# The place of two operand transpositions among the steps of an RWKV-7 scan on TensorE

## The chip, the cores and the metric

The kernel runs on one core of a Trainium2 chip. The metric is the device time of one execution in microseconds (us). TensorE (PE in the profile; PEld is its loading of weights) multiplies matrices into PSUM, VectorE (DVE) and ScalarE (ACT) work on the elements and copy out of PSUM, GpSimd (POOL) works on SBUF, and SyncE (SP) issues the transfers. Each engine works through its own instructions strictly in the order in which the program has them, and waits on semaphores for the others.

## The reference, cut to what matters

The program is a decoder trunk of two layers on 512 tokens of width 2048, all in 32-bit floats. Layer 0 has stick-breaking attention and a pooling mixer; layer 1 is RWKV-7 time mixing with 32 heads of 64. The part that the change touches is the recurrence of layer 1:

```python
def step(state, inp):
    r_t, w_t, k_t, v_t, kk_t, a_t = inp
    sa = jnp.einsum('bhvk,bhk->bhv', state, -kk_t)
    state = (state * w_t[:, :, None, :]
             + sa[..., None] * (kk_t * a_t)[:, :, None, :]
             + v_t[..., None] * k_t[:, :, None, :])
    return state, jnp.einsum('bhvk,bhk->bhv', state, r_t)
...
r = (xr @ w_r); k = (xk @ w_k); v = (xv @ w_v); g = (xg @ w_g)
...
o = wkv7_scan(r, decay, k, v, kk, a)
...
return o.astype(x.dtype) @ w_o
```

## The kernel before, in words

Layer 0, and the projections r, k and g of layer 1, take about the first 1430 us. Then comes the scan, which is what the change edits. It handles the 32 heads as 16 pairs and the 512 tokens as 8 chunks of 64. Within a chunk the recurrence becomes dense products. For each pair `p` the code has generators, whose pieces end at each `yield`:

- `chain(p)` is the serial part. Per chunk it has three steps: `xo` from the running state `M` and the operands (L1044, L1047) and its copy to `xs` by DVE and ACT (L1051, L1052); the product `sa` of `U` and `xs` (L1055) and its copy into `RS` by DVE (L1056); then `s1` (L1062) from `RS` and `BT`, the new state `M` by DVE (L1071, L1073) and the second half of `xo` (L1076).
- `gprod(p)` prepares a pair: it loads the operands `AR` and `BK` (L898, L900, 512 KB each), makes the products `g` of both (L908) and masks them into `Z` (L914) in four pieces, and transposes the eight blocks of `BK`, four at a time (`bt`, L920), each four copied into `BT` by ACT (L921). These last two pieces are the two transpositions of the title. `BK` has one buffer, so the load for the next pair waits until the second transposition of this pair has read it. `AR` has four buffers.
- `lanes(p)` inverts small blocks, almost wholly on DVE: `nd` by POOL (L950), its transposition `lt` (L955), `la` (L957), then fifteen steps of a product `pr` and a sum `uc` (L962, L963). `levels(p)` joins the blocks on TensorE (`q`, `c`: L1000, L1010) with additions into `U` (L1013, L1026).
- `vproj(p)` is the projection v of the pair, 512 columns wide (`vps`, L145 to L147 by a helper), its weights arriving as `wraw` (L154) and being split by ACT and POOL; `vprep(p)` transposes v (L937); `post(p)` normalises the output and multiplies by the gate.

The pieces are laid out in time by hand. A period has twelve positions, and one pair is begun in each period. In each position, `slot` first runs one step of each of the two chains that are alive, and then all pieces whose due time falls in that position. Since each chain takes three positions for a chunk, positions 0, 3, 6 and 9 hold `xo`, positions 1, 4, 7 and 10 hold `sa`, and positions 2, 5, 8 and 11 hold `s1`. The tuple `GP = (0.5, 9)` spreads the six pieces of `gprod` evenly over that stretch: at 0.5, 1.9, 3.3, 4.75 (the products g), 6.2 and 7.6 (the two transpositions). TensorE's order is exactly the written one; the orders of DVE, ACT, POOL and SP come out of a scheduler that works by priority and by what it reckons to be ready.

The first two pairs are prepared ahead of the loop; the other fourteen go through `plan_pair`.

Of the kernel before, what the change touches and what calls it, by code (L numbers as in the profile page):

```python
# [27 lines left out]

PO, LA, VP, LV, GP, VJ = (13.5, 20), (8, 15), (21.5, 25), (16, 24.5), (0.5, 9), (5.5, 17)
Q14, A13, B13, A14, B14, A15, B15, Q15 = (0, 3), (0.5, 5.5), (6, 12), (0, 10), (3, 12), (0, 9), (0.5, 11.5), (0, 11.5)


class Kernel:
# [809 lines left out]
    def scan(self, ctx, xv, first, mp, ld, ar_d, bk_d, bc_d, g_d, m_d):  # L845
# [29 lines left out]
        def vproj(p):  # L875

            unit = lambda k0: self.wunit(
                Wv[k0 * P:(k0 + 4) * P, p * P:(p + 1) * P].rearrange("(k p) n -> p k n", p=P), 4, P,
                eng=nc.gpsimd if p > 1 else None)
            ws = first if p == 0 else [unit(0)]  # L880
            ps = pv.tile([P, S], F32, tag="v", name="vps")
            for k in range(NK):
                if k % 4 == 0:
                    wh, wl = ws.pop(0)
                    if k + 4 < NK and not ws:
                        ws.append(unit(k + 4))
                self.mm3(ps, wh[:, k % 4, :], wl[:, k % 4, :], xv[k][:, 0, :], xv[k][:, 1, :], k == 0, k == NK - 1)
                if k % 2 and k < NK - 1:
                    yield
            vT = sets[p]["vT"] = tp.tile([P, S], F32, tag="vT", name="vT")  # L890
            nc.scalar.copy(vT, ps)  # L891
            yield

        def gprod(p):

            s = sets[p]
            AR = s["AR"] = ld.tile([P, 8, 2, 64], F32, tag="AR", name="AR", bufs=4)
            nc.sync.dma_start(AR.rearrange("p a b c -> p (a b c)"), ar_d[p])  # L898
            BK = ld.tile([P, 8, P], F32, tag="BK", name="BK")
            nc.sync.dma_start(BK.rearrange("p a b -> p (a b)"), bk_d[p])  # L900
            yield

            Z = s["Z"] = [st.tile([P, 8, P], F32, tag=f"Z{h}", name=f"Z{h}", bufs=4) for h in range(2)]
            for b in range(2):
                g = [aux("g").rearrange("p (c n) -> p c n", c=4) for _ in range(2)]
                for c in range(4):
                    for h in range(2):
                        mm(g[h][:, c, :], BK[half[h], 4 * b + c, :],  # L908
                           AR[half[h], 4 * b + c].rearrange("p a b -> p (a b)"), start=True, stop=True)
                    if c == 1:  # L910
                        yield
                for h in range(2):
                    mk = self.mk[:, 64 * (p % 2):64 * (p % 2) + P]
                    nc.vector.tensor_mul(Z[h][:, 4 * b:4 * b + 4, :], g[h], mk.unsqueeze(1).to_broadcast([P, 4, P]))  # L914
                yield
            BT = s["BT"] = st.tile([P, 8, P], F32, tag="BT", name="BT")
            for b in range(2):
                g = aux("bt")
                for c in range(4):
                    nc.tensor.transpose(g[:, c * P:(c + 1) * P], BK[:, 4 * b + c, :], self.ident)  # L920
                nc.scalar.copy(BT[:, 4 * b:4 * b + 4, :], g.rearrange("p (c n) -> p c n", c=4))  # L921
                yield

        def vprep(p):

            s = sets[p]
            bv = s["bv"] = tp.tile([P, S], F32, tag="bv", name="bv", bufs=3)
            nc.sync.dma_start(bv, bc_d[p])
            for q in range(4):
                nc.gpsimd.tensor_mul(bv[:, q * P:q * P + P], s["vT"][:, q * P:q * P + P], bv[:, q * P:q * P + P])  # L930

            RS = s["RS"] = st.tile([P, 8, 2, 64], F32, tag="RS", name="RS", bufs=3)
            nc.gpsimd.memset(RS[half[p % 2]], 0.0)
            yield
            g = aux("vt")
            for t in range(4):
                nc.tensor.transpose(g[:, t * P:(t + 1) * P], s["vT"][:, t * P:(t + 1) * P], self.ident)  # L937
            g5 = g.rearrange("p (t h n) -> p t h n", t=4, h=2)
            for par, rows in ((0, lo), (1, hi)):
                nc.scalar.copy(RS[half[1 - p % 2], par::2], g5[rows])  # L940
            yield
# [217 lines left out]
        todo = []  # L1159

        def plan(base, g, n, a, b):

            todo.extend((base + a + (b - a) * q / n, len(todo), g) for q in range(n))
# [12 lines left out]
        def hurry(g):  # L1176
            while True:
                with tc.high_priority(offset=400):
                    if next(g, g) is g:
                        return  # L1180
                yield

        def plan_pair(base, q, skip=0):

            gp = gprod(q)
            next(gp)
            plan(base, gp, 6, *GP)
            plan(base, hurry(lanes(q)) if q == 15 else lanes(q), 18, *LA)
            plan(base, hurry(levels(q)) if q == 15 else levels(q), 5, *LV)
            plan(base, vproj(q), 8, *VJ)  # L1190
            plan(base, vprep(q), 2, *VP)


        v, gp = vproj(0), gprod(0)
# [33 lines left out]
        for p in range(-1, 16):  # L1228
            at = 12 * (p + 1)
            if p + 3 < 16:  # L1230
                plan_pair(at, p + 3)
            if 0 <= p < 15:
                late = 1.2 if p in (13, 14) else 0
                plan(at, post(p), 6, PO[0] + late, PO[1] + late)
            if p == 13:
                plan(at, units(0, 1, 2), 3, *A13)
                plan(at, project(*both(0, 1, 2)), 6, *B13)
            if p == 14:
                plan(at, units(3, 4, 5, 6, 7), 5, *A14)
                plan(at, project(*both(3, 4, 5, 6, 7)), 10, *B14)  # L1240
                plan(at, project(*[(2, k) for k in range(3)]), 3, *Q14)
            if p == 15:
                plan(at, units(8, 9, 10, 11, 12, 13), 6, *A15)
                plan(at, project(*both(8, 9, 10, 11, 12, 13)), 12, *B15)
                plan(at, project(*[(2, k) for k in range(3, 10)]), 7, *Q15)
            B = chain(p + 1) if p < 15 else None
            slot(at, [c for c in (A, B) if c])
            A = B
# [91 lines left out]
```

## Time and profile before

| | us |
|---|---|
| median of three runs | 2084.72 |
| lowest and highest of them | 2082.19, 2085.89 |
| the profiled execution | 2082.21 |
| its span, first to last instruction | 2080.4 |
| TensorE busy in it | 2016.8 (97%) |
| VectorE busy | 1282.0 (62%) |
| ScalarE busy | 961.5 (46%) |
| GpSimd busy | 282.7 (14%) |

Between the span and the time of the execution lie 1.8 us. The shares are means over stages with different limits: most of the span is the large projections, in which TensorE never waits. A timeline row gives the start, the duration from the first to the last of the merged instructions, the engine, the line, the operation, the tiles (out<-in) with their sizes, the count, and in brackets the idle time ahead of it and who ended it.

### The profile page before, as it was taken

The numbers are of one execution on the slowest core, as the hardware profiler recorded it, in microseconds if no ns is written. First come the engines' busy times: TensorE is split into PE (matmuls) and PEld (weight loads), VectorE is DVE, ScalarE is ACT, GpSimd is POOL, SyncE is SP. The second block draws the span as 40 slices with busy tenths as digits, with TensorE's granted clock in tenths as the row PEclk, the third lists the DMA queues.
The fourth block names the chain that finished last, engine by engine and source line by source line (L and its number), as shares of the span: only waits on it lengthen the run. The fifth ranks groups of instructions, "written<-read, shape, count | busy, mean of one in ns | idle before, by whom it ended". The sixth has DMA issues, their size and how long they took to land.

```text
span 2080.4 us, 33934 instructions
## 1 busy us (share of the span) xinstructions
PE 2016.8 (97%) x13091; PEld 1637.4 (79%) x13091; DVE 1282.0 (62%) x2572; ACT 961.5 (46%) x1687; POOL 282.7 (14%) x550
## 2 busy tenths in 40 slices
PE   8999999999999998999999999999999999989996
PEld 7888888888888897777878888886777777767786
DVE  5344345444433357666866676668788888886436
ACT  3345445323322138654745564454555555564221
POOL 0000000000000000234000000013444444410003
PEclk9999999999999999999999999999999999999998
DMA  5222222233333353465365556542223332232733
GB/s 195 92 81 81 81 81 66 86 97 100 98 111 112 115 169 126 138 180 178 118 213 190 181 171 218 198 166 67 91 76 106 109 108 89 95 118 92 245 105 111
DMA packets 214034, 262.99 MB, mean 126 GB/s; under 512 B 15769, under 2 KB 161777, under 8 KB 213105
## 3 DMA queue, kind: packets, MB, share of 16 engines
q1 hardware_dynamic: 213872, 260.83, 38.6%
q8 instruction: 103, 1.69, 0.3%
q14 instruction: 59, 0.48, 0.1%
HBM read 214.32 MB, written 46.47 MB: 125 GB/s over the span
## 4 chain that ended last, share of the span: by engine, by line
PE 77%; DVE 14%; ACT 3%; issue 2%; DMA 2%; POOL 1%; SPq 0%; DVEq 0%; ACTq 0%; POOLq 0%
PE ga L145 16%; PE ga L146 16%; PE ga L147 16%; PE gb L506 4%; PE gb L508 4%; PE gb L507 4%; DVE pr L962 2%; PE vps L145 2%; DVE uc L963 1%; DVE M L1071 1%; PE vps L146 1%; PE vps L147 1%; DVE RS L1056 1%; PE g L908 1%; PE y L506 1%
## 5 line engine op out<-in xcount | busy, mean ns | idle before, releaser
L141 DVE TENSOR_TENSOR wlo<-wraw,whi 128x1024 fp32r<-128x1024 f32 (+1 forms) x268 | 314.1, 1175 | 467.3 <-ACT whi L137 464.0
L137 ACT CAST whi<-wraw 128x1024 fp32r<-128x1024 f32 (+1 forms) x324 | 303.0, 938 | 545.2 <-PE ga L146 297.9
L145 PE MATMUL ga<-mx,whi 128*128 128x512 f32 x768 | 299.9, 391 | 3.2 <-ACT mx L137 3.2
L146 PE MATMUL ga<-mx,whi 128*128 128x512 f32 x768 | 300.4, 391 | 1.6 <-DVE mx L141 1.6
L145 PE MATMUL ga<-x,whi 128*128 128x512 f32 x768 | 300.5, 391 | 0.1
L147 PE MATMUL ga<-mx,wlo 128*128 128x512 f32 x768 | 300.3, 391 | 0.0
L147 PE MATMUL ga<-x,wlo 128*128 128x512 f32 x768 | 299.5, 390 | 0.5 <-DVE wlo L141 0.5
L146 PE MATMUL ga<-x,whi 128*128 128x512 f32 x768 | 299.2, 390 | 0.0
L508 PE MATMUL gb<-wlo,mixed 128*128 128x512 f32 (+1 forms) x576 | 197.4, 344 | 2.8 <-DVE wlo L141 2.8
L506 PE MATMUL gb<-whi,mixed 128*128 128x512 f32 (+1 forms) x576 | 198.0, 344 | 1.6 <-DVE s L457 1.6
L507 PE MATMUL gb<-whi,mixed 128*128 128x512 f32 (+1 forms) x576 | 197.5, 343 | 0.0
L145 PEld LDWEIGHTS ga<-mx,whi 128*128 128x128 f32 x768 | 144.8, 189 | 36.3 <-ACT mx L137 3.6
L146 PEld LDWEIGHTS ga<-mx,whi 128*128 128x128 f32 x768 | 144.9, 189 | 32.9 <-DVE mx L141 1.9
L147 PEld LDWEIGHTS ga<-mx,wlo 128*128 128x128 f32 x768 | 144.8, 189 | 30.6
L147 PEld LDWEIGHTS ga<-x,wlo 128*128 128x128 f32 x768 | 144.2, 188 | 31.2 <-DVE wlo L141 1.0
L145 PEld LDWEIGHTS ga<-x,whi 128*128 128x128 f32 x768 | 144.2, 188 | 29.6 <-ACT whi L137 0.4
L146 PEld LDWEIGHTS ga<-x,whi 128*128 128x128 f32 x768 | 144.3, 188 | 29.1
L141 POOL TENSOR_TENSOR wlo<-wraw,whi 128x128 fp32r<-128x128 f32 x224 | 100.3, 478 | 221.9 <-ACT whi L137 195.1
L508 PEld LDWEIGHTS gb<-wlo,mixed 128*128 128x128 f32 x576 | 109.4, 190 | 16.4 <-DVE wlo L141 3.7
L506 PEld LDWEIGHTS gb<-whi,mixed 128*128 128x128 f32 x576 | 109.5, 190 | 16.0 <-DVE s L457 3.3
L507 PEld LDWEIGHTS gb<-whi,mixed 128*128 128x128 f32 x576 | 109.6, 190 | 12.5
L145 PE MATMUL vps<-mx,whi 128*128 128x512 f32 x256 | 113.4, 443 | 0.8 <-ACT vT L891 0.8
(333 smaller groups left out, 3347.7 us busy)
## 6 DMA issues: line engine op xcount, KB each, us to landing
wraw<-in_ev_w_in SPq DMA_DIRECT2D x96, 512.0 KB, 3.6
wraw<-in_ev_w_out SPq DMA_DIRECT2D x32, 512.0 KB, 3.6
wraw<-in_od_w_k SPq DMA_DIRECT2D x32, 512.0 KB, 4.7
wraw<-in_od_w_r SPq DMA_DIRECT2D x32, 512.0 KB, 3.4
wraw<-in_od_w_g SPq DMA_DIRECT2D x32, 512.0 KB, 3.8
wraw<-in_od_w_v SPq DMA_DIRECT2D x64, 256.0 KB, 2.8
ar_d<-pAR SPq DMA_DIRECT2D x16, 512.0 KB, 2.6
bk_d<-pBK SPq DMA_DIRECT2D x16, 512.0 KB, 3.2
```

The source lines that it names most:

```text
L137: self.nc.scalar.copy(hi, src)
L141: (eng or self.nc.vector).tensor_sub(lo[:, sl], src[:, sl], hi[:, sl].bitcast(F32))
L145: mm(ps, ah, bh, start=start, stop=False)
L146: mm(ps, ah, bl, start=False, stop=False)
L147: mm(ps, al, bh, start=False, stop=stop)
L506: mm(ps, ah, bh, start=start, stop=False)
L507: mm(ps, al, bh, start=False, stop=False)
L508: mm(ps, ah, bl, start=False, stop=stop)
L908: mm(g[h][:, c, :], BK[half[h], 4 * b + c, :], AR[half[h], 4 * b + c].rearrange("p a b -> p (a b)"), start=True, stop=True)
L962: nc.vector.tensor_mul(q, uc[:, :t, :t], la[:, t, :t].unsqueeze(1).to_broadcast([P, t, t]))
L963: nc.vector.tensor_reduce(uc[:, :t, t], q, AX.X, ALU.add)
L1056: nc.vector.tensor_copy(RS[a, c], sa[a])
```

## The change

`GP` becomes a list of six times, one for each piece, instead of a stretch. The four products g keep their positions (0, 1, 3 and 4). The first transposition goes from position 6 to position 7 (it was due at 6.2, now at 7.6), and the second from position 7 to position 10 (from 7.6 to 10.5).

```diff
-PO, LA, VP, LV, GP, VJ = (13.5, 20), (8, 15), (21.5, 25), (16, 24.5), (0.5, 9), (5.5, 17)
+PO, LA, VP, LV, GP, VJ = (13.5, 20), (8, 15), (21.5, 25), (16, 24.5), (0.5, 1.9, 3.3, 4.75, 7.6, 10.5), (5.5, 17)
...
             gp = gprod(q)
             next(gp)
-            plan(base, gp, 6, *GP)
+            todo.extend((base + x, len(todo), gp) for x in GP)
             plan(base, hurry(lanes(q)) if q == 15 else lanes(q), 18, *LA)
```

On TensorE, position 6 of a period, the difference between the two programs (- is before, + is changed; bt is the transposition, vps the v projection behind it):

```order
 L1047 MATMUL xo<-RS,Z_11009 64x64
 L1047 MATMUL xo<-RS,Z_11151 64x64
-L920 MATMUL bt<-ident,BK 128x128 x4
 L145 MATMUL vps<-mx,whi 128x512
 L146 MATMUL vps<-mx,whi 128x512
```

The four blocks that stood between xo and the v projection are gone from there. Position 7 reads the same in both programs (sa, c, four blocks bt, s), only that these are now the first four blocks of the pair and no longer the last.

On TensorE, position 10 of the same period (sa of the two chains, c a product of levels):

```order
 L1055 MATMUL sa<-xs_10977,U 64x128
 L1055 MATMUL sa<-xs_10978,U 64x128
-L1000 MATMUL c_12086<-U,q_12053 32x32 x16
+L920 MATMUL bt<-ident,BK 128x128 x4
+L1000 MATMUL c_12086<-U,q_12047 32x32 x16
 L1062 MATMUL s_12105<-RS,BT 64x64 x2
 L1076 MATMUL xo<-RS,Z_11008 64x64
```

Four blocks now stand between sa and c. Both differences come fourteen times, once for each pair that `plan_pair` places.

On SP, which issues the transfers, from the gate's load ldg on, in one period before:

```order
L1087 DMA ldg<-g_d 128x512
L900 DMA BK<-bk_d 128x1024
L898 DMA AR<-ar_d 128x1024
L154 DMA wraw<-in_od_w_v 128x4x128 x4
```

and in the same place of the changed program:

```order
L1087 DMA ldg<-g_d 128x512
L154 DMA wraw<-in_od_w_v 128x4x128
L898 DMA AR<-ar_d 128x1024
L900 DMA BK<-bk_d 128x1024
L154 DMA wraw<-in_od_w_v 128x4x128 x3
```

The load of BK has gone behind one load of weights and behind that of AR. DVE's and ACT's rows are laid out anew by the scheduler too: on ACT the second copy BT stands behind the position's cast whi; on DVE the steps pr and uc lie differently around the copies xs, RS and M, by one or two steps either way. POOL's order is the same.

## Rows read from the trace of the kernel before

**Rows 1.** The page: busy us of each engine, share of the span, instructions.
```profile
PE 2016.8 (97%) x13091; PEld 1637.4 (79%) x13091; DVE 1282.0 (62%) x2572; ACT 961.5 (46%) x1687; POOL 282.7 (14%) x550
```

**Rows 2.** Windows, the scan: us, then busy of PE, PEld, DVE, ACT, POOL, granted clock.
```profile
1430.00:1830.00 400.00, 384.14 (x4889) 288.19 (x4889) 341.33 (x1107) 229.79 (x591) 172.25 (x340) 1.00 0.30 95
```

**Rows 3.** Waits of PE from 1430 to 1830: total us, times, longest.
```profile
PE s L1062 <- DVE RS L1056: 8.8, 22, 0.7
...
PE c L1000 <- ACT q L1021: 0.3, 1, 0.3
```

**Rows 4.** Timeline of PE, positions 6 and 7 of one period.
```profile
1585.44 0.65 PE L920 MATMUL bt<-ident,BK 128*128 128x128 f32 x4
1585.85 0.48 PE L145 MATMUL vps<-mx,whi 128*128 128x512 f32 x1
...
1587.42 0.44 PE L1055 MATMUL sa<-xs,U 128*64 128x128 f32 x4
...
1588.63 0.66 PE L920 MATMUL bt<-ident,BK 128*128 128x128 f32 x4
1589.21 0.45 PE L1062 MATMUL s<-RS,BT 128*64 128x64 f32 x8
```

**Rows 5.** Timeline of PE, position 10 and on: typical, first, last, and behind c.
```profile
1594.45 0.44 PE L1055 MATMUL sa<-xs,U 128*64 128x128 f32 x4
1594.82 0.69 PE L1000 MATMUL c<-U,q 32*32 32x32 f32 x32
1596.23 0.34 PE L1062 MATMUL s<-RS,BT 128*64 128x64 f32 x4 [0.72 <-DVE RS L1056]
...
1599.31 0.72 PE L908 MATMUL g<-AR,BK 64*128 64x128 f32 x8
...
1480.59 0.34 PE L1062 MATMUL s<-RS,BT 128*64 128x64 f32 x4 [0.65 <-DVE RS L1056]
...
1802.27 0.34 PE L1062 MATMUL s<-RS,BT 128*64 128x64 f32 x4 [0.36 <-DVE RS L1056]
...
1831.45 0.54 PE L1000 MATMUL c<-U,q 32*32 32x32 f32 x22 [0.67 <-ACT q L1021]
```

**Rows 6.** Timeline of ACT and DVE and PE, position 6 of two neighbouring periods.
```profile
1585.74 0.71 DVE L955 STREAM_TRANSPOSE lt<-nd 128x512 f32<-128x512 f32 x1 [1.63 <-POOL nd L950]
1586.65 0.47 ACT L1052 COPY xs<-xo 64x64 f32<-64x64 f32 x2 [1.14 <-DVE xs L1051]
...
1616.61 0.45 ACT L1052 COPY xs<-xo 64x64 f32<-64x64 f32 x2 [1.56 <-DVE xs L1051]
...
1616.97 0.59 PE L1055 MATMUL sa<-xs,U 128*64 128x128 f32 x4
```

**Rows 7.** Landing: BK in 1400-1420, 1440-1480, 1500-1800; AR in 1500-1800.
```profile
DMA to landing us min/median/max: 3.4/3.5/3.6
...
DMA to landing us min/median/max: 3.6/3.8/4.1
...
DMA to landing us min/median/max: 4.4/5.1/5.6
...
DMA to landing us min/median/max: 4.0/4.8/5.8
```

**Rows 8.** Timeline of SP, the loads of one period.
```profile
1588.90 0.41 SPq L1087 DMA_DIRECT2D ldg<-g_d  x1
1589.37 0.42 SPq L900 DMA_DIRECT2D BK<-bk_d  x1
1591.89 0.32 SPq L898 DMA_DIRECT2D AR<-ar_d  x1
```

**Rows 9.** Timeline of PE, later waits of s for RS; ACT at position 11.
```profile
1632.40 0.28 PE L1062 MATMUL s<-RS,BT 128*64 128x64 f32 x2 [0.28 <-DVE RS L1056]
1639.53 0.28 PE L1062 MATMUL s<-RS,BT 128*64 128x64 f32 x2 [0.19 <-DVE RS L1056]
1596.84 0.54 ACT L1079 COPY O<-xo 64x128 f32<-64x128 f32 x2 [1.22 <-PE xo L1076]
```

## Prediction

> **What bounds the kernel now.** I read the page first: TensorE is busy 97% of the span, so whatever moves the end must be idle time of TensorE or work added to it [rows 1]. Then the windows: in the scan, from 1430 to 1830 us, TensorE is busy 384 of 400 us and DVE 341, at a granted clock of 1.00 [rows 2]. So 16 us are all that could be gained there, and DVE is close behind. The list of waits says whom TensorE waits for: 8.8 us in 22 waits of s for RS, which DVE copies, and 0.3 us of c for ACT's q [rows 3]. Last I read the timeline where blocks bt are taken out and put in. Ten of the 22 waits stand at position 10, right behind c; read from the timeline they come to 5.9 us, the first 0.65, the last 0.36, most 0.5 to 0.74 [rows 5]. Positions 6 and 7 show no wait of TensorE [rows 4].
>
> **The change, part by part.** The number of instructions stays the same everywhere; only places change.
>
> Out of position 6. The four blocks set back the next work by 1585.85 - 1585.44 = 0.41 us [rows 4], 14 x 0.41 = 5.7 us. But what follows the v projection there is sa, which needs xs from ACT. In the period at 1585, ACT's copies end at 1586.65 + 0.47 = 1587.12 and sa starts at 1587.42 [rows 4, 6]: no more than 0.30 us can be taken. In the neighbouring period they end at 1616.61 + 0.45 = 1617.06 while sa has begun at 1616.97, and takes 0.59 instead of 0.44 us because its second half waits [rows 6]: nothing can be taken. xs is late because DVE must first do lt, which stood 1.63 us waiting for POOL's nd [rows 6], and no transposition moves nd. In the trace six periods are like the first, five like the second, and three early ones have room for the whole 0.41. That is 6 x 0.30 + 3 x 0.41 = 3.0 us gained; the other 2.7 us turn into new waits of sa for xs.
>
> Position 7 holds sa, c, four blocks and s, as before: nothing.
>
> Into position 10. Ahead of s, four blocks cost 1589.21 - 1588.63 = 0.58 us [rows 4], 14 x 0.58 = 8.1 us. They fill the wait behind them: of the ten waits for RS seven are longer than 0.58 and give 4.1 us, the other three (0.52, 0.29, 0.36) give 1.2; in two periods it is c that waits for q, 0.30 us in one and 0.67 in the other [rows 3, 5], which gives 0.9. Together 6.1 us, so that position 10 costs 8.1 - 6.1 = 2.0 us net. The longer stay in position 10 delays nothing that DVE needs earlier than now, since s starts within 0.1 us of its old time in the typical period: 1594.45 + 0.37 + 0.58 + 0.69 = 1596.09 against 1596.23.
>
> ACT's copy BT goes with the blocks. It falls into the 1.22 us in which ACT idles ahead of O [rows 9], and costs nothing; if that cover were gone, O and the copies of v behind it would be late by one such copy, and with them the products g that reuse their PSUM.
>
> The load of BK. This is the wait that the change adds. BK has one buffer, and its load starts when the last blocks have been read. Before, that was 1588.63 + 0.66 = 1589.29 [rows 4]; SP issued at 1589.37 [rows 8], and g needed it at 1599.31 [rows 5], 9.9 us later. Now the blocks end 0.37 + 0.66 = 1.03 us after sa of position 10 starts, and SP, which will be standing at this load, issues some 0.03 us later. g is due after 0.37 + 0.58 + 0.69 us for sa, bt and c, and 1599.31 - 1596.23 = 3.08 us from s to g [rows 5], thus 4.72 us after that start. So the load has 4.72 - 1.06 = 3.66 us. Behind it on SP are only loads of weights, which wait for POOL's splits anyway, and behind g on TensorE stand v's projection, sa and everything else. How long does it take? With little else on the way 3.4 to 4.1 us (four loads); with the transfers m_d and ldg issued within a microsecond ahead of it 4.4 to 5.6, median 5.1 (eleven); and AR, issued 2.5 us behind BK, took 4.0 to 5.8 [rows 7, 8]. In the new order AR goes out some 3.6 us ahead and ldg over 6 us ahead, so the nearest rows are the first four. I take 3.8 us, toward their upper end: g then waits 0.14 us, 13 times (the last pair has no load behind it), 1.8 us. About half of that comes back, since in half the periods s waits for RS twice after g, 0.28 and 0.19 us [rows 9], and DVE sets those times: 0.9 us remain. The ends are 0 (3.66 us or less) and, at 5.1 us, a wait of 1.44 us, of which even with 0.47 given back 13 x 0.97 = 12.6 us are lost.
>
> The Trainium skill, "DMA: Bandwidth & Descriptors", section "Issuing engines are not separate DMA queues", says that all transfers run on the same 16 DMA engines and interleave. Here 512 KB took 3.4 us with the queue clear and 5.1 us in company, which agrees. By that rule AR's tail would stretch BK too, and the term would lie nearer to 12.6 than to 0.9 us.
>
> DVE's and ACT's new order. The steps pr and uc are the same work; they shift by one or two places, in some periods with RS earlier, in four with la or a step ahead of xs. Nothing in the trace shows this order. I cost it at nothing, between -3 us (the 8.8 us of waits for RS less the 5.9 at position 10) and +5 us (a wait like that of 0.72 us [rows 5] once in every second of the fourteen periods).
>
> Sum: -3.0 + 2.0 + 0.9 = -0.1 us. The profiled execution took 2082.21 us, 1.8 of them outside its span of 2080.4, which the change does not touch; it lies 2.5 us under the median of the runs. From its own time the sum gives 2082.1, from the median 2084.6. I predict 2084.6 us: no change. Within 0.2%, 4 us, this kernel's runs cannot tell a change from none.
>
> **Rivals.** The first ends on the slower side: the load of BK comes too late in every period. Mechanism: a single buffer, freed at position 10, needed at position 12. It decides from the point where the load takes about 4.5 us: then g waits 1.06 + 4.5 - 4.72 = 0.84 us, 0.37 after what DVE gives back, 4.8 us over 13 periods; at 5.1 us it is 12.6 us. Its middle is +9 us, 2094 us. For it: eleven of the fifteen loads in the scan took 4.4 us or more [rows 7]. Against it: those had ldg right ahead of them [rows 8], and the new place has not.
>
> The Trainium skill, "Perfetto Trace Analysis", section "Optimization Strategy", names this as a pattern: the same gap repeated on the engine that should be saturated can mean too few buffers for the next tile. No run here shows it yet.
>
> The second: the gain comes whole. If the new order on DVE brings xs and RS to TensorE in time, position 6 gives its 5.7 us, position 10 costs only 2.0, and of the remaining 2.9 us of waits for RS 2 go as well: -5.7 + 2.0 - 2.0 = -5.7 us, 2079 us. For it: in most periods of the new order RS at position 10 stands ahead of one more step pr or uc. Against it: DVE runs without a gap from lt to the next period, so a copy made earlier makes a step later, and lt itself hangs on POOL [rows 6].
>
> The third: time only changes its place. TensorE's wait goes from position 10 to position 6, and BK's load lands just in time: between -3 and +3 us. This is my forecast's own case, with DVE as the pace.
>
> **How the numbers follow.** No change, with the load in time or nearly: 0.55, its own range 2081 to 2089. BK late: 0.23, from 2089 to 2100. Gain whole: 0.17, from 2077 to 2081. DVE's order costing 5 us by itself: 0.05. Slower by over 0.2% is BK late and the bad order, less the part of the former under 4 us: 0.26. Faster by over 0.2% is the whole gain and a small tail of the main case: 0.19. Within: 0.55. The range for 8 in 10 cuts a tenth at either end: 2079 to 2096 us.
>
> **What the profile would show.** Right: s at position 10 no longer waits for RS; new waits of sa for xs at position 6, about 0.1 us (0.41 - 0.30) in one kind of period and 0.4 in the other; BK issued about 1 us after sa of position 10 starts and landing 3.5 to 4 us later; g at position 0 waiting 0.2 us at most; the scan from 1430 to 1830 as long as before. Wrong: g waiting for BK by half a microsecond or more in each period, or position 6 without waits and a scan shorter by over 4 us.

## The result, and the profile after

The changed kernel is slower: a median of 2091.76 us in 13 runs (2087.46 to 2096.65), against 2082.19 us for the kernel before in its 13 runs of the same comparison. The ratio is 1.0047, 95% interval [1.0037, 1.0057], that is 7.7 to 11.9 us. The forecast was no change, 2084.6; the time lies in its range, on the side of the rival with the late load. The profiled execution happens to be the slowest of the 13, 2096.65 us with a span of 2094.9. So a second execution was profiled as well (2091.32 us, span 2089.6), which stands for the typical one.

The page of the changed kernel, busy us of each engine, answers to [rows 1]:

```profile
PE 2026.8 (97%) x13091; PEld 1643.3 (78%) x13091; DVE 1286.2 (61%) x2572; ACT 962.7 (46%) x1687; POOL 281.8 (13%) x550
```

The number of instructions is the same, yet TensorE is busy 10.0 us longer. The same matmuls took longer, and the windows say most of why. First the scan, in the profiled execution, then in the second one (columns as in [rows 2]; the third figure from the end is the granted clock):

```profile
1430.00:1830.00 400.00, 380.48 (x4689) 284.44 (x4688) 333.98 (x1070) 222.79 (x570) 164.22 (x325) 0.98 0.29 90
```

```profile
1430.00:1830.00 400.00, 381.12 (x4765) 284.53 (x4765) 338.35 (x1080) 226.24 (x581) 168.50 (x332) 1.00 0.30 91
```

Before, the clock was 1.00 there and TensorE busy 384.14 us [rows 2]. So two things were added: waits, in both executions, and a lower clock, far more in the slower one.

The waits of TensorE from 1430 to 1830 us in the profiled execution (total us, times, longest) answer to [rows 3]:

```profile
PE g L908 <- DMA BK<-bk_d: 6.1, 5, 2.5
PE q L1000 <- ACT DT L973: 3.7, 3, 1.6
PE s L1062 <- DVE RS L1056: 3.0, 9, 0.6
PE sa L1055 <- ACT xs L1052: 2.8, 5, 1.6
PE vps L145 <- ACT vT L891: 2.4, 4, 0.8
```

and the lines of the kernel before that the prediction had not shown beside [rows 3]:

```profile
PE q L1000 <- ACT DT L973: 2.3, 4, 0.6
PE sa L1055 <- ACT xs L1052: 1.8, 3, 1.3
...
PE vps L145 <- ACT vT L891: 0.8, 1, 0.8
```

Read as a balance, s no longer waits for RS at position 10 and c no longer for q: 8.8 + 0.3 - 3.0 = 6.1 us less. In exchange g waits 6.1 us for BK, and q, sa and vps wait 8.9 us for ACT instead of 4.9. That is 4 us more waiting in the scan, and it is made of other waits: of the 22 short ones, none over 0.7 us, 9 are left, and longer ones have come. In the second execution the list reads 4.2 us for BK in five waits, the longest 1.2, and the same 3.7, 2.8 and 2.4 us for DT, xs and vT.

A period with its load in time shows the two moves as the prediction drew them. This is TensorE's timeline at position 7 and then 10 of one pair, to the next pair's first g, answering to [rows 4, 5]:

```profile
1626.83 0.44 PE L1055 MATMUL sa<-xs,U 128*64 128x128 f32 x4
1627.20 0.91 PE L1010 MATMUL c<-U,q1z 64*48 64x32 f32 x32
1628.04 0.65 PE L920 MATMUL bt<-ident,BK 128*128 128x128 f32 x4
...
1633.86 0.44 PE L1055 MATMUL sa<-xs,U 128*64 128x128 f32 x4
1634.23 0.65 PE L920 MATMUL bt<-ident,BK 128*128 128x128 f32 x4
...
1635.43 0.34 PE L1062 MATMUL s<-RS,BT 128*64 128x64 f32 x4
...
1638.50 0.79 PE L908 MATMUL g<-AR,BK 64*128 64x128 f32 x8
```

None of these rows carries a wait. The period's first g starts at 1609.25 (its row below), so it took 29.25 us; the same one before took from 1599.31 [rows 5] to 1628.79, 29.48. It is 0.23 us shorter, where the forecast's -3.0 + 2.0 makes 0.07 a period: the sign agrees, and one period shows no more. Nor is it free of waits: s waits 0.23 us for RS and vps 0.69 for vT, where before q waited 0.57 for DT and s 0.52 for RS.

What differs more is a few periods that go wrong. Here the load of BK takes its time, and what follows costs on top of the wait (columns of the timeline; in brackets the idle time ahead and its releaser):

```profile
1576.74 1.32 PE L908 MATMUL g<-AR,BK 64*128 64x128 f32 x8 [2.50 <-DMA BK<-bk_d]
1577.99 0.79 PE L145 MATMUL vps<-mx,whi 128*128 128x512 f32 x1
1578.58 0.63 PE L146 MATMUL vps<-mx,whi 128*128 128x512 f32 x1
1579.01 0.63 PE L147 MATMUL vps<-mx,wlo 128*128 128x512 f32 x1
...
1609.25 0.79 PE L908 MATMUL g<-AR,BK 64*128 64x128 f32 x8
...
1610.31 0.39 PE L146 MATMUL vps<-mx,whi 128*128 128x512 f32 x1
1610.54 0.40 PE L147 MATMUL vps<-mx,wlo 128*128 128x512 f32 x1
```

Eight products g take 1.32 us instead of 0.79, and the products vps follow each other at 0.43 us instead of 0.23: half speed, 1.2 instead of 2.4 GHz. The windows of the same execution put the clock to it, behind the five waits of 1.16 (xo for M, at 1434), 1.63 (sa for xs, 1472), 2.50, 1.31 (q for DT, 1592) and 1.58 us (q for DT, 1742):

```profile
1436.00:1440.00 4.00, 3.99 (x23) 3.10 (x24) 2.14 (x5) 0.66 (x2) 1.76 (x3) 0.59 0.03 6
...
1474.00:1478.00 4.00, 4.00 (x26) 3.02 (x26) 3.68 (x14) 1.51 (x4) 1.02 (x3) 0.57 0.22 66
1576.00:1580.00 4.00, 3.26 (x13) 2.68 (x14) 1.31 (x7) 0.40 (x2) 0.00 (x0) 0.58 0.01 4
1592.00:1596.00 4.00, 4.00 (x54) 3.55 (x55) 2.16 (x5) 1.55 (x4) 2.21 (x4) 0.71 0.22 64
1596.00:1600.00 4.00, 4.00 (x62) 2.92 (x60) 3.19 (x9) 1.07 (x4) 1.75 (x5) 0.86 0.49 143
...
1744.00:1748.00 4.00, 4.00 (x28) 2.78 (x26) 2.12 (x8) 1.47 (x4) 0.00 (x0) 0.59 0.17 66
```

4 us at 0.59 cost 4 x 0.41 = 1.6 us. The five together are 4 x (0.41 + 0.43 + 0.42 + 0.29 + 0.14 + 0.41) = 8.4 us. The kernel before has waits of 1.2 and 1.3 us too, at 1434 and 1471, and its clock stays at 1.00 behind both; in the second execution of the changed kernel only the 1.58 us wait was followed by a fall. So such a wait is followed by half speed in one execution and not in another, and this makes most of the spread: over the 13 runs the mean clock goes from 0.992 (the two fastest, 2087.46 and 2088.41) to 0.988 (2096.65 and 2095.77). As time lost, span x (1 - clock), that is 16.7 to 25.1 us, 8.4 of the 9.2 us between fastest and slowest, each good to 1 us, since the clocks are given to three digits.

The windows of 400 us above don't hold the same work, since the changed kernel is further behind at 1830 us. From the first product g behind 1430 us to that of the last pair they do (before, the profiled execution, the second one):

```profile
1430.70:1805.40 374.70, 359.47 (x4599) 269.93 (x4596) 319.19 (x1038) 215.20 (x554) 162.04 (x320) 1.00 0.30 95
```

```profile
1430.50:1819.40 388.90, 369.48 (x4596) 276.56 (x4595) 323.64 (x1038) 216.78 (x554) 162.18 (x320) 0.98 0.30 92
```

```profile
1429.90:1812.60 382.70, 364.37 (x4595) 272.33 (x4594) 323.60 (x1038) 216.40 (x554) 162.08 (x320) 1.00 0.31 93
```

The profiled execution takes 14.2 us longer for it, 4.2 of idle time and 10.0 of longer work; the second takes 8.0 longer, 3.1 and 4.9. Of the longer work the clock is 8.4 and 1.6 us, and 2.2 are the blocks themselves at the prediction's own prices: 0.58 us ahead of c instead of 0.41 ahead of vps, in 13 periods. At the scan's end the last ot waits 3.6 us for O instead of 2.5 and q 0.7 for uc, 1.8 us in both, and the second execution has one more fall of the clock there (0.59 from 1876 to 1880 us). In return the kernel before has a fall from 1948 on (0.68 and 0.89 in two windows of 4 us, 1.7 us) that neither of these has. That accounts for the 14.5 and 9.2 us in the spans to about 1 us.

### The profile page after: what moved, and what is told of

Read it like the earlier page. It is cut to its first block, busy times and chain, and to the rows that moved or that the text cites. A ratio compares the mean times of both kernels' runs of the same rounds, so it can differ in the third digit from the quotient of the medians.

```text
span 2094.9 us, 33936 instructions
## 1 busy us (share of the span) xinstructions
PE 2026.8 (97%) x13091; PEld 1643.3 (78%) x13091; DVE 1286.2 (61%) x2572; ACT 962.7 (46%) x1687; POOL 281.8 (13%) x550
## 4 chain that ended last, share of the span: by engine, by line
PE 81%; DVE 11%; DMA 3%; ACT 3%; issue 2%; POOL 1%; SPq 0%; DVEq 0%; ACTq 0%; POOLq 0%
PE ga L146 15%; PE ga L147 15%; PE ga L145 15%; PE gb L506 4%; PE gb L508 4%; PE gb L507 4%; PE vps L145 3%; PE vps L146 2%; PE vps L147 2%; PE g L908 1%; PE xo L1044 1%; DMA BK<-bk_d 1%; PE q L1000 1%; PE sa L1055 1%; DVE wlo L141 1%
## 5 line engine op out<-in xcount | busy, mean ns | idle before, releaser
L506 PEld LDWEIGHTS gb<-whi,mixed 128*128 128x128 f32 x576 | 109.1, 190 | 15.4 <-DVE s L457 2.8
```

Of the source, the lines that this page charges most:

```text
L506: mm(ps, ah, bh, start=start, stop=False)
```

## The experiments

All medians are of runs beside the kernel before on the same chip; ratios are to that. E12's one run has none.

| kernel | median us | ratio [95%] |
|---|---|---|
| changed (7, 10) | 2091.76 | 1.0047 [1.0037, 1.0057] |
| e1: (7, 10), two buffers for BK | 2091.60 | 1.0045 [1.0031, 1.0059] |
| e2: before (6, 7), two buffers | 2085.47 | 1.0010 [1.0001, 1.0019] |
| e3: first alone (7, 7) | 2084.95 | 1.0014 [1.0005, 1.0023] |
| e4: second alone (6, 10) | 2087.45 | 1.0025 [1.0016, 1.0034] |
| e5: (6, 10), two buffers | 2086.22 | 1.0019 [1.0009, 1.0030] |
| e6: e1 with DT raised | 2090.81 | 1.0034 [1.0021, 1.0046] |
| e7: before with DT raised | 2083.58 | 1.0001 [0.9992, 1.0011] |
| e8: (7, 11) | 2145.22 | 1.0284 [1.0262, 1.0306] |
| e9: (7, 11), the wait filled | 2112.93 | 1.0143 [1.0129, 1.0158] |
| e10: (7, 9) | 2087.77 | 1.0028 [1.0019, 1.0037] |
| e11: second alone (6, 9) | 2078.82 | 0.9986 [0.9978, 0.9995] |
| e12: changed, second profile | 2091.32 | one run |
| e13: (7, 9) with DT raised | 2085.09 | 1.0015 [1.0006, 1.0024] |
| e14: second alone (6, 8) | 2079.82 | 0.9986 [0.9976, 0.9996] |

**Is it the load, or the rest?** E1 takes the reason for the late load away, e2 is its control on the kernel before. The tile ml and one weight tile wo share BK's place and get the second buffer with it (the edit at wo isn't shown).

```diff
-            BK = ld.tile([P, 8, P], F32, tag="BK", name="BK")
+            BK = ld.tile([P, 8, P], F32, tag="BK", name="BK", bufs=2)
...
-                    ml = ld.tile([P, 2, S], F32, tag="BK", name="ml")
+                    ml = ld.tile([P, 2, S], F32, tag="BK", name="ml", bufs=2)
```

> The changed kernel with two buffers for BK (and for the tile ml that shares its place), so that the load of BK for the next pair need not wait for the transposition at position 10. Theory T1, the load of BK lands too late and TensorE's clock falls in the longest of these waits: the loss goes, 2076 to 2084 us, ratio to the kernel before 0.997 to 1.001, and no wait of g for BK is left. Theory T2, the loss comes from position 6 left without cover (sa waiting for xs) and from the new order on DVE and ACT: it stays 6 to 10 us slower, ratio 1.003 to 1.005, with the same waits of q for DT and of sa for xs as in the changed kernel.

> The kernel before with two buffers for BK and ml: the control for e1. BK has 9 us to spare there, so T1 expects no change from it in the scan; the tile ml of the output projection may gain 1 or 2 us at the end of the scan. Ratio 0.998 to 1.001 by both theories. What e1 gains beyond this control is due to the load of BK in its late place.

In e1 no wait of g for BK is left, and by its median it is as slow as the changed kernel (five runs; the profiled one, 2086.63 us, is the fastest of them). In its list, for the same stretch, the lines of q, sa and vps stand word for word as in the changed kernel's (3.7, 2.8 and 2.4 us for ACT), and s waits

```profile
PE s L1062 <- DVE RS L1056: 5.3, 16, 0.8
```

With xo's 1.2 us for M, as before, e1's list comes to 15.4 us, and that of the kernel before to 15.4 as well: what position 10 saved is spent on other operands. The second buffer by itself costs 1.0010 (e2: a wait of 2.4 us at the scan's end, where the first ml is issued at 1798 us instead of 1825). So by the medians the two moves with the load in time cost 1.0045 - 1.0010, about 7 us (4 to 11 by the intervals), and the late load the rest, 2 to 3 us. In the traces the load's share is a little larger: for the same work the second execution's scan takes 382.7 us and e1's 379.4, with one fall of the clock in each. That the load is all of it is refuted.

**One move at a time.**

```diff
-GP = (0.5, 1.9, 3.3, 4.75, 7.6, 10.5)
+GP = (0.5, 1.9, 3.3, 4.75, 7.55, 7.6)    # e3
+GP = (0.5, 1.9, 3.3, 4.75, 6.2, 10.5)    # e4, and e5 with two buffers
```

> Only the first transposition moves (6 to 7); the second stays at position 7, so BK is freed where it was. T1: no loss of the kind seen, 2079 to 2085 us, ratio 0.998 to 1.001; new waits of sa for xs at position 6 of up to 0.4 us, paid back where s waits at position 10. T2 (position 6 without cover is what costs): 2086 us or more, ratio 1.002 or more.

> Only the second transposition moves (7 to 10); the first stays at position 6. BK is freed as late as in the changed kernel. T1: slower by as much as the changed kernel, ratio 1.003 to 1.007, with waits of g for BK in a good part of the 13 periods. T2: position 6 keeps its cover, so most of the loss goes, ratio 0.999 to 1.002.

E4's list of waits:

```profile
PE g L908 <- DMA BK<-bk_d: 5.4, 5, 1.4
...
PE q L1000 <- ACT DT L973: 0.8, 1, 0.8
```

The first move alone costs 1 to 5 us, the second alone 3 to 7, and the second carries the BK waits, as it must. Both lie between the ranges of the two theories. E3 has the long wait of q for DT (1.58 us), e4 has not. The product of both ratios, 1.0039, is near the 1.0047 of the two together.

> The second transposition alone at position 10, with two buffers for BK (and for ml, which shares its tag), so that the next load no longer waits for the blocks at position 10. Theory T1 (what the second move costs is the late BK load alone): the five waits of g for BK, 5.2 us in the kernel with the same positions and one buffer, are gone, the waits of the state products for RS behind position 10's blocks stay gone, and the time falls from 2087.5 to about 2081 to 2083 us, below the 2085.5 of the kernel before with two buffers. Rival T2 (the order of DVE and ACT costs what the moves lose): it stays at 2086 to 2089 us, with the lost time in waits for DT, vT, xs or RS.

E5 has no wait for BK, and still 7.4 us of waits for RS in 22 (before: 8.8 in 22): some 2.7 us of them stand at position 7, which has lost its blocks, instead of position 10, and the others behind the products g. It came out in the rival's range. Against e2 it costs 1.0019 - 1.0010, 2 us, which the intervals don't tell from nothing. So by the medians the 5.4 us of waits for BK in e4 are worth some 3 us; by the traces some 4 (378.3 us for the same work in e4, 374.0 in e5, without a fall of the clock in either), since s waits 6.2 us for RS in e4 instead of 7.4.

**Is it DT's place on ACT?** ACT's timeline in the changed kernel, ahead of the 1.31 us wait of q at 1592, shows the order e, vT, whi, DT, O, m, DT:

```profile
1587.03 0.91 ACT L969 ACTIVATE e<-uc,hm 128x256 f32<-128x256 f32 x2 [0.98 <-DVE uc L963]
1587.96 0.59 ACT L891 COPY vT<-vps 128x512 f32<-128x512 f32 x1
1588.44 0.62 ACT L137 CAST whi<-wraw 128x512 fp32r<-128x512 f32 x1
1589.23 0.77 ACT L973 ACTIVATE DT<-tb,qm 128x256 f32<-128x256 f32 x1 [0.17 <-DVE tb L971]
1590.03 0.54 ACT L1079 COPY O<-xo 64x128 f32<-64x128 f32 x2
1590.60 0.69 ACT L1066 ACTIVATE m<-M,pcs 128x128 f32<-128x128 f32 x2
1591.20 0.73 ACT L973 ACTIVATE DT<-tb,qm 128x256 f32<-128x256 f32 x1
```

TensorE ends its last vps at 1590.67 and stands until the second half of DT is there, at 1591.93; it was begun 1.2 us after the first half had ended, with O and m between. The kernel before has O, O between the halves in every second period from 1610 us on, and m never. The edit raises e, tb and DT in the scheduler's eyes (lines behind it move down by one):

```diff
+            with self.tc.high_priority(offset=400):
                 for h in range(2):
                     nc.scalar.activation(e[:, :, h, :], uc, ...)
                 ...
                     nc.scalar.activation(DT[...], tb[...], ...)
```

> Both transpositions moved, two buffers for BK and ml (2091.6 us so far), and in every pair e, tb and DT, the last steps of lanes, are issued at a raised priority, so that ACT does DT ahead of the two m copies in every pair; nothing else is edited. Theory T2 (with the load in time, what is left of the loss is ACT's new order, which sets O, O, m, m ahead of DT while q waits for DT): the three waits of q for DT of 0.76, 1.33 and 1.58 us go to 0.5 or less each, and the time falls by 3 us or more, to 2085 to 2088.5. Rival (the waits for DT only stand where another wait would, or the granted clock carries the loss): 2090 to 2092 us, the same as without the edit.

> The kernel before, with e, tb and DT at a raised priority in every pair, as its own control. T2: the four waits of q for DT of 0.57 us go (ACT then does DT, DT, O, O in each pair), 2.3 us, and the time falls to 2079 to 2081 us, unless DVE's tb pushes an RS or M copy back. Rival: no change, 2081.5 to 2083, the waits come back at the state products as waits for RS.

E6's waits:

```profile
PE sa L1056 <- ACT xs L1053: 5.0, 9, 1.6
...
PE q L1001 <- ACT DT L974: 1.5, 4, 0.4
```

The waits for DT go from 3.7 to 1.5 us, those for xs from 2.8 to 5.0, and the time does not clearly answer (1.0034 against 1.0045, intervals that overlap; it lies in the rival's range). E7 says the same: the waits for DT are gone there, and the time is that of before. The rival was nearer: where operands come this close to their use, hurrying one made the next one late.

**How much is the clock?** E8 makes the wait for BK happen in every period; e9 keeps it and gives TensorE something to do in it, transpositions of the identity into g's tiles, which the products overwrite.

```diff
+GP = (0.5, 1.9, 3.3, 4.75, 7.6, 11.5)    # e8 and e9
...
+                if b == 0 and 3 <= p:        # e9 alone, ahead of g
+                    for c in range(20):
+                        nc.tensor.transpose(g[c % 2][:, c // 2 % 4, :], self.ident, self.ident)
```

> The changed kernel with the second transposition at position 11 instead of 10: the BK load is issued one position later, 2.4 us of a period of 29.1 us over 12 positions, so of the 3.66 us that it had to spare about 1.2 are left. T1: g waits for BK in each of 13 periods, by 2.2 to 2.4 us where the load takes 3.4 to 3.6 us and more where it takes longer, some 30 to 40 us in all, and the granted clock falls behind such waits, which adds 5 to 15 us: 2118 to 2140 us. Rival (the load is issued in time anyway, or the wait replaces others that go): under 2105 us.

> The second transposition at position 11, as in the run of 2145.2 us, where g waited for BK 12 times by 3.33 us (40 us) and the time rose by 62 us. The edit puts 20 transpositions of the identity into the same PSUM tiles ahead of g's first product from the fourth pair on (about 0.145 us each at full speed, 2.9 us of work in the wait; it writes nothing that is read). Theory T3 (a long wait of TensorE is followed by a stretch at 1.2 GHz, whose slow matmuls are lost on top of the wait): the wait is nearly as long but filled, the granted clock stays at 1.00 behind g, and the time falls by 15 to 25 us, to 2118 to 2130, though work was added. Rival (the 62 us are the waits alone, the lower clock is their result on paper): 2143 us or more, since nothing is taken away and 13 x 2.9 us of work are added.

The waits of g for BK from 1430 to 1870 us, and the clock from 1430 to 1880, in e8:

```profile
PE g L908 <- DMA BK<-bk_d: 44.0, 13, 3.9
```

```profile
1430.00:1880.00 450.00, 396.66 (x4716) 297.73 (x4714) 332.87 (x1080) 224.72 (x576) 164.26 (x329) 0.91 0.27 81
```

and in e9, with one of its filled waits:

```profile
PE g L911 <- DMA BK<-bk_d: 12.5, 13, 1.7
```

```profile
1430.00:1880.00 450.00, 426.43 (x5329) 327.30 (x5327) 356.81 (x1162) 243.81 (x625) 173.26 (x345) 0.99 0.30 88
```

```profile
1582.54 2.44 PE L908 MATMUL g<-ident 128*128 128x128 f32 x20
1586.04 0.71 PE L911 MATMUL g<-AR,BK 64*128 64x128 f32 x8 [1.06 <-DMA BK<-bk_d]
```

E9 lost as much time to the load as e8: 13 x 2.44 us of idle work and 12.5 us of waits are 44.2 us, against 44.0. But its clock is 0.99 instead of 0.91, and it costs 32 us instead of 62, each against the kernel before on its chip, with work added. So half of what e8 costs is the slow matmuls behind the waits. Both expectations were too small in size: the load had 0.57 us to spare at position 11, not 1.2, and the clock was worth 30 us, not 15 to 25.

**The load in time without a second buffer.**

```diff
+GP = (0.5, 1.9, 3.3, 4.75, 7.6, 9.5)     # e10, and e13 with DT raised
+GP = (0.5, 1.9, 3.3, 4.75, 6.2, 9.5)     # e11
+GP = (0.5, 1.9, 3.3, 4.75, 6.2, 8.5)     # e14
```

> The changed kernel with the second transposition at position 9 instead of 10, one buffer for BK: both stand behind sa, and the load is issued one position earlier, with about 6 us to spare instead of 3.66. T1: no wait of g for BK but for a load over 5.5 us, and of the 9.6 us that the change lost the 4 to 6 for the load come back: 2084 to 2088 us. T2 (ACT's and DVE's new order, with waits for DT, vT and xs) says what is left: 1 to 4 us above the kernel before, since this order sets O, O ahead of the second DT in every other period as before, and nowhere m. If the load were all of the loss: 2081 to 2083 us.

> The first transposition stays at position 6 and the second moves from 7 to 9, one buffer. The load is in time (T1), and ACT does DT, DT ahead of O, O in every period, so the four waits of q for DT of 0.57 us are gone (T2): both theories expect 2080 to 2083 us, that is no loss against the kernel before, and a gain of up to 2 us. A rival, that any move of a transposition behind sa costs by itself, by waits of the products at the place it leaves: 2084 to 2088 us.

> The changed kernel once more, for a second execution's trace. T1: g waits for BK in 3 to 7 of 13 periods, again 4 to 8 us in all, but not in the same periods, since the length of a load differs from execution to execution. T3: behind the waits of TensorE over about 1.2 us (q for DT, g for BK, sa for xs) the granted clock stands at half speed in some and not in others, and the time of this execution, between 2087 and 2097 us, goes with how many of these there are: 2 to 3 fewer than the profiled one had where it is near 2090.

E10 still costs 4 to 8 us, with one wait for BK in the scan; a little over what was expected. E11 is the first kernel here that beats the one before, by 1 to 5 us, a little more than expected. The waits of TensorE in e11, and those in e10:

```profile
PE s L1062 <- DVE RS L1056: 7.3, 22, 0.8
PE sa L1055 <- ACT xs L1052: 1.5, 2, 1.2
```

```profile
PE s L1062 <- DVE RS L1056: 6.2, 14, 0.7
PE sa L1055 <- ACT xs L1052: 3.2, 8, 1.6
PE q L1000 <- ACT DT L973: 2.9, 5, 0.6
PE g L908 <- DMA BK<-bk_d: 1.5, 1, 1.5
```

They differ only in the first transposition, at 6 or at 7. Taking it away from position 6 saves 1.1 us of waits for RS and adds 1.7 for xs and 2.9 for DT. The second profile of the changed kernel (e12) has five waits for BK of 0.6 to 1.2 us, and one fall of the clock in the scan instead of five, where two or three fewer were expected. The late loads were expected in other periods, but they are the same five: issued at 1511, 1540, 1571, 1694 and 1756 us in the first execution, at 1508, 1538, 1568, 1687 and 1749 in the second. Four of these five periods are late in e4 as well. So it is not chance from one execution to the next that picks them.

> Both transpositions behind sa (positions 7 and 9, one buffer: 2087.8 us, while the second alone at 9 gave 2078.8), with e, tb and DT at a raised priority, so that ACT does DT, DT ahead of O, O in every period, as it does of itself in the kernel with the second alone at 9; nothing else is edited. T2 (the first move costs through the place of DT on ACT): q's waits for DT, 3.06 us in six, go, and the time falls by 4 us or more toward 2079 to 2083. Rival (the block at position 6 was cover for xs and for q of the chain behind it; whoever takes it away pays at the next operand that DVE or ACT bring, in whatever order ACT works): the waits for DT go, those of sa for xs grow by as much, and the time stays at 2086 to 2089 us.

> The first transposition at position 6, the second at position 8, one buffer. If what made position 9 good (2078.8 us) is that the block left position 7 and filled the wait for RS at 9 or 10, position 8 has to give less, since the wait of s for RS at position 10 is open again: 2080 to 2083 us. Rival (it is ACT's order alone, DT ahead of O in every period, which this kernel has too): 2078 to 2080 us, the same as at 9.

With DT first, e13 has no wait for DT and 4.6 us for xs, and keeps a cost of 1 to 5 us:

```profile
PE sa L1056 <- ACT xs L1053: 4.6, 6, 1.6
```

So DT's place is worth some 3 us of e10's 6 (the two intervals overlap a little), and the other 3 go with the missing cover at position 6, where xs is waited for 4.6 us instead of e11's 1.5. Both theories hold in part. E14 gains the same 1 to 5 us as e11, so the gain does not hang on filling the wait at position 10: it hangs on the block leaving position 7 while position 6 keeps its own, in an order where ACT does both halves of DT before O (no wait for DT is left in e11 from 1430 to 1830 us). E7 showed that this order alone, with the blocks at 6 and 7, gains nothing. E11 and e14 are the versions to keep; which of the two is not decided.

## Why the prediction was wrong, step by step

It failed in three places: the new order was priced at nothing, the load by a single landing time, and the clock was not in the sum. That the time lies in the range is owed to the range's width, not to the mechanism.

- **What bounds the kernel**: right. TensorE is at 97% in both, and DVE and ACT bring their copies so close to the use that a microsecond taken from one wait shows up in another (e1, e6, e13).
- **Out of position 6, -3.0 us**: holds in a period with its load in time, not as a sum. The expected waits of sa for xs are there in two places (0.2 and 0.4 us), but xs, DT and vT together rose from 4.9 to 8.9 us. Moving this block costs against every kernel without that move: e3 against before (1.0014), e10 against e11 (1.0028 and 0.9986), e1 against e5 (1.0045 and 1.0019).
- **Into position 10, +2.0 us**: right as far as position 10 goes, where no wait for RS is left. That the move costs 2 us by itself is not shown: e5 against e2 gives 2 us within the noise, and with other waits for RS than the sum had.
- **The load of BK, +0.9 us**: a step that failed. The cover was right, the price was not. In the period of 1634 us the blocks end at 1634.88, BK is issued at 1634.91 and g starts 3.59 us later without waiting; the forecast had 0.03 and 3.66 us. The loads took 3.4 us at the least and 3.5 in the median, but 3.9, 4.2, 4.5 and 5.0 in four, and one, issued at 1570.58, was still waited for at 1576.74, 6.2 us later. I took one value, 3.8, for all thirteen, where only the tail over 3.6 us costs anything: 6.1, 4.2 and 5.4 us of waits in three traces, worth 2 to 4 us by e1 and e4. The slowest load was issued while AR was on its way (issued at 1567.01, landed after 5.32 us). The Trainium skill, "DMA: Bandwidth & Descriptors", section "Issuing engines are not separate DMA queues", describes such interleaving, and this load agrees. But a load at 1664.15, with AR under way for another 1.0 us, took 3.4, and one at 1755.57, with AR landed 0.2 us before, took 5.0, so the rule doesn't say which loads are slow. Nor does the order on SP: two of the five late ones (1570.58 and 1693.53) had m_d and ldg 4.1 to 4.6 us ahead, where the forecast had ldg over 6 us ahead in every period, but e4 is late in the same two with ldg 6.4 us ahead or more.
- **DVE's and ACT's new order, 0 us (-3 to +5)**: this is the step that failed most by the medians. With "Nothing in the trace shows this order. I cost it at nothing" I took a value inside a range for lack of a row. The two moves with the load in time cost about 7 us (e1 against e2) where position 6, position 10 and this term together were to give -1.0. By the means of the clock some 2 of the 7 are half speed (22.1 us lost in e1's five runs, 20.3 in e2's eleven); most of the rest reads in the trace as waits that should have gone. The sum had 6.1 us of them go at position 10 and 2.7 come at position 6; in e1's trace as much came as went. In the trace, then, this step and the load's price missed by about as much, 3 to 4 us each. ACT puts O and m ahead of DT in two periods, vT waits stand in three more, and each hits TensorE, which has no slack. That ACT's order changes could be read before the run; what it would cost could not.
- **The clock, not in the sum**: I priced a wait at its length. Behind five waits of 1.16 to 2.50 us half speed cost 8.4 us more; two of the five, 1.16 and 1.63, have their like in the kernel before (1.16 and 1.26 us), without a fall. Over its 13 runs the mean clock is 0.9904, against 0.9913 in the 26 runs of before beside e1, 20.1 against 18.0 us lost (18.6 to 19.0 in the other sets of before): 1 to 2 us of the median, 8 in the slowest run.
- **The rival "BK late in every period", 2094 us**: near in time, for another reason. The load was late in 5 of 13 periods, and by the medians it is the smaller part. The Trainium skill, "Perfetto Trace Analysis", section "Optimization Strategy", names the same gap repeated on the engine that should be saturated as a possible sign of too few buffers. E8 fits it, with a gap in all 13 periods; in the changed kernel the gaps stood in five, and the second buffer of e1 removed them and not the loss.

Not settled: what makes the load late in just these periods, why e1's median lies 5 us above its one trace, and how the 3 us of position 6 divide between xs and what follows from it.

## What to carry to other kernels

Work taken from one slot of a tight pipeline and put into another costs through what the other engines then do in a different order; read that order for every operand that the saturated engine waits for, and price it from both sides instead of at nothing. Several short waits of TensorE are cheaper than one long wait of the same sum, because half speed may follow the long one: in the scans here it followed waits of 1.16 us and more, and never waits of 1.0 us or less. A transfer that just fits has to be priced by the tail of its landing times, period by period, not by their median.

## What the runs showed of the hardware

- A 512 KB load landed in 3.4 to 3.6 us in most periods and in 3.9 to some 6 us in five of thirteen, and the same five were late in the next execution.
- TensorE ran at half speed behind waits as short as 1.16 us, in some executions and not in others. Filling 13 waits of 3.4 us with matmuls that nobody reads kept the clock at 0.99 instead of 0.91 and was worth 30 us in e9, although the wait itself was not shortened.
